# Sixteen weight pieces on ScalarE's queue, a first mixer without order edges, and q and k chains that share tables and roots

## The chip, the cores and the metric

The kernel runs on one core of one Trainium2 chip. The metric is the device time of one execution in microseconds (us), as the median of several runs. Float32 data go through TensorE as float32r, and most operands are split into a high and a low part, so that one product is three matmuls.

## The reference

One decoder layer on x of 1024 tokens by 1024 columns:

```python
x = x + 0.5 * swiglu(rms_norm(x, ffn1_norm), ffn1_w_gate, ffn1_w_up, ffn1_w_down)
h = rms_norm(x, mix_norm)
q, k, v, qi, ki, wi, u = split(h @ w_in)
q = rope(rms_norm(q, q_norm)); k = rope(rms_norm(k, k_norm))
qi = rope(qi); ki = rope(ki)
attn = dsa_attention(q, k, v, qi, ki, wi, top_k=256)
pooled = multiscale_pool(u) @ pool_w * pool_scale
x = x + concat(attn, pooled) @ w_out
x = x + 0.5 * swiglu(rms_norm(x, ffn2_norm), ffn2_w_gate, ffn2_w_up, ffn2_w_down)
```

There are 8 heads of 64. Each query attends to the 256 keys that the indexer (qi, ki, wi) scores highest.

## The kernel before

The tokens are cut into two halves of 512 (h = 0 and 1). FFN 1's gate and up projections run first for both halves (`expand`), and in the same loop the mixer's weights w_in and w_out are split and stored in DRAM as 56 pieces of 128 x 2 x 512 (`p_dr`, by `make_piece`): 8 each for q, k, v and the indexer, 8 for the pooling channels, 16 for the output projection (p_dr 40 to 55). Every later use of a piece is a load by `get_piece` (L229) into a buffer: tag "bw" has 3 buffers, and the first output projection borrows the 4 buffers "sc", which are the softmax tiles of attention as well.

Then the halves are interleaved by Python generators. `fill(main, other)` (L911) advances the main work by a step and then as much of the other work as pays for it. The main work is first `first_mixer` (L951): norm, index projection, scores, `projections` (pooling mixer, k, q, v) with the top-k search, `attention` of half 0, `out_proj` of half 0, then `norm_transposed(0, 2)`. The other work is `down(1)` of FFN 1 and then `second_mixer_opens` (L983), which does the norm, index projection and q, k, v projections of half 1. Later the second mixer is the main work, and FFN 2 fills.

Each engine runs its instructions in one fixed order, which a scheduler writes out when the program is built: it takes instructions by priority as they become ready in its own model of time. `tc.issue_after(mark)` adds an edge that keeps an instruction from being put ahead of `mark` on the mark's engine; on other engines the edge does nothing. In `fill` (L922) the flag `strict[0]` sets such edges: the other work's instructions on TensorE go behind the main work's matmuls of two steps before. `first_mixer` sets the flag at L965, ahead of attention; the second mixer sets it too (L1002). `second_mixer_opens` waits for the flag (L987) before it starts the index projection.

`attention` (L794) takes 4 head pairs in turn, for each 2 blocks of queries and 2 heads: 16 steps for half 0, 8 over 256 keys and 8 over 512. A step is the logits (`lg`, PE), mask and maximum (L823, DVE), exponentials and scaling (L830, L833 on ACT, L834 on DVE), transposes of the probabilities (`tp`, PE), their split (L851 ACT, L852 DVE), the product with the values (`pv`, PE) and its store in `o` (L860 ACT, L861 DVE). The second part of a step runs behind the logits of the next one.

`qk_proj` (L606) multiplies 8 pieces into four banks (`pj`), one for 128 tokens each, and then for each of the four tiles runs a chain: copy from the bank and square (L615, L616, ACT), sums of 64 (L618, DVE), the inverse root of 8 head norms (`rstd_of`: L145, L146, POOL), scaling (L620, DVE), the rotation with a table of gains times cosines and sines made for this tile (L611, POOL; L622 DVE, L623 and L624 POOL, L625 DVE), transposes (`qt`, PE, into the only bank of tag "pv"), split (L630 ACT, L631 DVE) and two stores (L637, SP). The table's tag "st2" has one buffer.

`out_proj` (L518) of half 0 takes 16 pieces, 8 for each half of the columns, into banks `op` of tags ba, ba, bt and pv; 12 matmuls use one piece. The pieces are issued on SP's DMA queue. Behind the sixth piece's matmuls it traces `fetch_x` (L540), which brings half 0's x back in two loads of 1 MB, with an edge behind the last piece's load on SP (`last_sp[0]`). `norm_transposed(0, 2)` squares and scales the four tiles of x and transposes them for FFN 2 (`ba` and `bt`, PE).

Of the kernel before, what the change touches and what calls it, by code (L numbers as in the profile page):

```python
# [10 lines left out]
F32 = mybir.dt.float32  # L11
# [3 lines left out]
AF = mybir.ActivationFunctionType  # L15
ALU = mybir.AluOpType
AX = mybir.AxisListType

S = 1024
D = 1024  # L20
# [4 lines left out]
NH = 8  # L25
HD = 64
# [6 lines left out]
HIGH = 10_000_000  # L33
# [4 lines left out]
def hybrid_layer(ctx: ExitStack, tc: tile.TileContext, x, ffn1_norm, ffn1_w_gate, ffn1_w_up,  # L38
                 ffn1_w_down, mix_norm, w_in, q_norm, k_norm, pool_w, pool_scale, w_out,
                 ffn2_norm, ffn2_w_gate, ffn2_w_up, ffn2_w_down, c_rope, c_diag, c_count, out):  # L40
    nc = tc.nc
# [2 lines left out]
    dr = ctx.enter_context(tc.tile_pool(name="dr", bufs=1, space=bass.MemoryType.DRAM))  # L44

    BUFS = {"XA": 4, "XB": 4, "x8": 4, "w": 5, "qm": 2, "a": 4, "bw": 3, "R": 4, "sc": 4, "mk": 6, "t": 2,
            "st": 4, "sel": 1, "sm": 3, "st2": 1}
    PBUFS = {"fg": 3, "pv": 1, "ba": 2, "bt": 2}
    uid = [0]

    def t(tag, shape, dt=F32, role=None):
        uid[0] += 1
        return sb.tile(shape, dt, name=f"{role or tag}{uid[0]}", tag=tag, bufs=BUFS.get(tag, 1))
# [5 lines left out]
    def f(ap):  # L59
        return ap.bitcast(F32)  # L60
# [23 lines left out]
    ki = sb.tile([128, S], F32R, name="ki")  # L84
    wi = sb.tile([128, 8, 4], F32, name="wi")
    halo = sb.tile([128, 4, 16], F32, name="halo")
    mhalf = sb.tile([128, 8], F32, name="mhalf")
    nc.vector.memset(mhalf, -0.5)
    nc.vector.memset(halo, 0.0)

# [50 lines left out]


    def rstd_of(ss, n, width):
        r = t("st", [128, 8])
        nc.gpsimd.tensor_scalar(r[:, :n], ss, 1.0 / width, EPS, op0=ALU.mult, op1=ALU.add)  # L145
        nc.gpsimd.tensor_tensor(r[:, :n], r[:, :n], mhalf[:, :n], op=ALU.pow)  # L146
        return r
# [78 lines left out]
        for l in range(2):  # L226
            nc.sync.dma_start(p_dr[i][:, l, :a * b], f(part[l][:, :a * b]))

    def get_piece(i, n=512, tag="bw"):  # L229
        w = t(tag, [128, 2, 512], F32R, "bw")  # L230
        last_sp[0] = nc.sync.dma_start(f(w[:, :, :n]), p_dr[i][:, :, :n]).ins
        return w[:, :, :n]


# [283 lines left out]
    def out_proj(h, region, last):  # L518

        mt = {}  # L520
        for k in (4, 5, 6, 7, 0, 1, 2):
            if k % 2 == 0:
                pair = t("X" + region, [128, 2, 2, HALF], F32R)
                n = 1 if k == 2 else 2
                nc.gpsimd.dma_start(pair[:, :n].rearrange("p k l c -> p k (l c)"),
                                    m_dr[h][k:k + n].rearrange("k p l c -> p k (l c)"))
            mt[k] = [pair[:, k % 2, l] for l in range(2)]
        mt[3] = last
        for c in range(2):
            banks = [bank(tag, "op") for tag in ("ba", "ba", "bt", "bt" if h else "pv")]  # L530
            for n, k in enumerate((4, 5, 6, 7, 0, 1, 2, 3)):
                with tc.issue_after(last_raw[0]) if c == 0 and n >= 3 else nullcontext():
                    wt = get_piece(P_O + 2 * k + c, tag="bw" if h else "sc")
                hi, lo = mt[k]
                for i in range(4):
                    tok = slice(i * 128, (i + 1) * 128)
                    mm3(banks[i], hi[:, tok], lo[:, tok], wt[:, 0], wt[:, 1], n == 0, n == NK - 1)
                if c == 0 and n == 5:
                    with tc.issue_after(last_sp[0]):
                        fetch_x(h)  # L540
                yield 0.0 if h else 1.0
            for i in range(4):
                xo = x_at(h, i)[:, c * 512:(c + 1) * 512]
                nc.vector.tensor_add(xo, banks[i], xo)
            yield 1.0
# [59 lines left out]

    def qk_proj(h, hT, cs, which, says, want, home, tags):  # L606
        banks = yield from proj(hT, P_QKV + 8 * which, 512, says, want, tags)
        for i in range(4):
            s = t(home, [128, D], role="qk")
            tab = t("st2", [128, 2, HD])  # L610
            nc.gpsimd.tensor_mul(tab, gqk[:, which], cs[:, i])  # L611
            n = s[:, 512:].rearrange("p (h d) -> p h d", d=HD)
            o = s[:, :512].rearrange("p (h d) -> p h d", d=HD)
            with tc.high_priority(offset=HIGH):
                nc.scalar.copy(s[:, 512:], banks[i])  # L615
            nc.scalar.activation(s[:, :512], s[:, 512:], AF.Square)  # L616
            ss = t("st", [128, 8])
            nc.vector.reduce_sum(ss, o, axis=AX.X)  # L618
            r = rstd_of(ss, 8, HD)
            nc.vector.tensor_mul(n, n, r[:, :, None].to_broadcast([128, NH, HD]))  # L620
            m = t("mk", [128, 512], role="qm").rearrange("p (h d) -> p h d", d=HD)
            nc.vector.tensor_mul(o, n, tab[:, 0:1].to_broadcast([128, NH, HD]))  # L622
            nc.gpsimd.tensor_mul(m[:, :, 0:32], n[:, :, 32:64], tab[:, 1:2, 0:32].to_broadcast([128, NH, 32]))  # L623
# [287 lines left out]
    def fill(main, other):  # L911

        due, marks = 0.0, []
        while True:
            try:
                due += next(main)
            except StopIteration as e:
                return e.value
            marks.append(last_pe[0])
            mark = marks[max(0, len(marks) - 1 - LAG)]  # L920
            while due > 0.0:
                with tc.issue_after(mark) if strict[0] else nullcontext():  # L922
                    got = next(other, None)
                due = 0.0 if got is None else due - got

# [25 lines left out]
    def first_mixer():  # L951
# [9 lines left out]
        for i in range(2):  # L961
            causal_mask(i, masks[i])
        yield from both(projections(0, hT, cs, wanted, 0.0, ("sc", "sc"), MINE), search(0, masks, [2, 3], sc),
                        1.3, 3.0)
        strict[0] = True  # L965
        last = yield from attention(0, masks, "A")
        yield from out_proj(0, "A", last)

# [98 lines left out]
```

## Time and profile before

| | |
|---|---|
| median of 3 runs | 1988.53 us (1986.66 to 1991.15) |
| profiled execution | 1991.77 us, its span 1990.0 us |
| PE busy | 1890.9 us, 95% of the span |
| DVE, ACT, POOL busy | 1182.9, 816.5, 409.1 us |
| mean granted TensorE clock | 0.980 of full speed |

The span is cut into stretches in which the busy time of each engine, the granted clock and the DMA engines' share are read; that shows where TensorE, busy 95% overall, is not. The waits name for each instruction that stood idle what released it. The mean length of an instruction comes from the groups by line and shape. Matmuls overlap, so a matmul's price is the distance from one start to the next rather than its own duration.

### The profile page before, as it was taken

To read this page: it belongs to the slowest core of one execution; us is meant where nothing else is said; L and a number is where in the kernel's file an instruction comes from. 1 tells how busy PE (TensorE), PEld (TensorE's weight loads), DVE (VectorE), ACT (ScalarE), POOL (GpSimd) and SP (SyncE) were. 2 spreads that over 40 slices of the span, in tenths; PEclk is the share of its full clock that TensorE was granted. 3 is DMA by queue.
4 is the path that set the end of the run, shared out by engine and by line. 5 is a ranking of instruction groups with operands and counts; after the bars stand their busy time and mean duration, and the time that the engine had idled before them with its cause. 6 is when DMAs were issued, how large, how long until landed. Compare 5 with 4: busy or idle time off the path is not lost.

```text
span 1990.0 us, 24221 instructions
## 1 busy us (share of the span) xinstructions
PE 1890.9 (95%) x8640; PEld 1558.5 (78%) x8640; DVE 1182.9 (59%) x2204; ACT 816.5 (41%) x1518; POOL 409.1 (21%) x419
## 2 busy tenths in 40 slices
PE   5899999999999999978898999999999999999999
PEld 3688888887878788766676888878888788888887
DVE  6955755654566498646525579997775253444344
ACT  6334333332334254255403458837665133322331
POOL 5654544540001014422412001101100000000000
PEclk9999999999999999988998999999999999999999
DMA  5266656667345736697767544645543542333332
GB/s 158 91 205 211 198 166 200 206 223 288 117 127 167 233 117 203 190 224 182 233 228 213 128 129 130 160 116 118 137 130 101 191 139 85 107 100 89 96 106 74
DMA packets 224393, 314.20 MB, mean 158 GB/s; under 512 B 34192, under 2 KB 143888, under 8 KB 224272
## 3 DMA queue, kind: packets, MB, share of 16 engines
q1 hardware_dynamic: 205904, 281.19, 45.0%
q0 software_dynamic: 18368, 31.46, 7.5%
q8 instruction: 68, 1.11, 0.2%
q14 instruction: 53, 0.43, 0.1%
HBM read 242.84 MB, written 69.76 MB: 157 GB/s over the span
## 4 chain that ended last, share of the span: by engine, by line
PE 86%; DVE 5%; DMA 4%; ACT 2%; POOL 1%; issue 1%; SPq 1%; DVEq 0%; POOLq 0%; ACTq 0%
PE fg L67 30%; PE dn L67 23%; PE pj L67 7%; PE bt L67 6%; PE ba L67 5%; PE pv L67 5%; PE op L67 4%; DMA bw<-p_dr 2%; PE pu L67 2%; PE lg L67 2%; PE tp L70 1%; DVE B L193 1%; DMA rawd<-in_ffn_w_down_dram 1%; DVE w L193 1%; DMA rawa<-a_dr 0%
## 5 line engine op out<-in xcount | busy, mean ns | idle before, releaser
L67 PE MATMUL dn<-wd,a 128*128 128x512 f32 x2112 | 508.0, 395 | 12.5 <-DVE x L455 4.9
L67 PEld LDWEIGHTS dn<-wd,a 128*128 128x128 f32 x2112 | 396.5, 189 | 98.5 <-DVE x L455 6.2
L67 PE MATMUL fg<-XA,w 128*128 128x512 f32 x1056 | 257.4, 393 | 0.0
L67 PE MATMUL fg<-XB,w 128*128 128x512 f32 x1056 | 240.3, 389 | 0.0
L67 PEld LDWEIGHTS fg<-XB,w 128*128 128x128 f32 x1056 | 198.3, 188 | 41.1
L67 PEld LDWEIGHTS fg<-XA,w 128*128 128x128 f32 x1056 | 195.5, 188 | 39.7
L192 ACT CAST w<-rawe 128x512 fp32r<-128x512 f32 x176 | 108.2, 620 | 176.5 <-PE fg L67 120.1
L193 DVE TENSOR_TENSOR w<-x,w 128x512 fp32r<-128x512 f32 x110 | 112.2, 1021 | 113.5 <-ACT w L192 109.0
L193 DVE TENSOR_TENSOR w<-rawe,w 128x512 fp32r<-128x512 f32 x176 | 121.2, 695 | 94.8 <-ACT w L192 94.5
L192 ACT CAST wd<-rawd 128x512 fp32r<-128x512 f32 x176 | 108.0, 620 | 153.0 <-PE dn L67 104.1
L193 DVE TENSOR_TENSOR wd<-rawd,wd 128x512 fp32r<-128x512 f32 x176 | 119.9, 690 | 64.2 <-ACT wd L192 62.3
L67 PE MATMUL fg<-B,w 128*128 128x512 f32 x420 | 105.4, 400 | 13.0 <-DVE B L193 10.0
L455 DVE SCALAR_TENSOR_TENSOR x<-dn,x 128x512 f32<-128x512 f32 x96 | 65.1, 689 | 70.7 <-PE dn L67 70.4
L67 PEld LDWEIGHTS fg<-B,w 128*128 128x128 f32 x420 | 79.7, 192 | 31.7 <-DVE B L193 11.8
L192 ACT CAST p<-praw 128x512 fp32r<-128x512 f32 (+1 forms) x56 | 33.6, 599 | 170.2 <-DMA praw<-in_w_in_dram 70.8
L453 DVE TENSOR_TENSOR x<-dn,x 128x512 f32<-128x512 f32 x96 | 64.0, 686 | 65.4 <-PE dn L67 64.9
L67 PE MATMUL pj<-bw,XB 128*128 128x512 f32 (+1 forms) x384 | 92.6, 392 | 8.3 <-DMA bw<-p_dr 4.5
L193 POOL TENSOR_TENSOR p<-praw,p 128x512 fp32r<-128x512 f32 (+1 forms) x56 | 72.9, 1302 | 134.0 <-ACT p L192 134.0
L67 PE MATMUL ba<-B,w 128*128 128x512 f32 x396 | 94.2, 390 | 0.0
L67 PE MATMUL pj<-bw,XA 128*128 128x512 f32 (+1 forms) x384 | 87.4, 378 | 4.6 <-DMA bw<-p_dr 4.6
L67 PEld LDWEIGHTS pj<-bw,XB 128*128 128x128 f32 x384 | 71.8, 201 | 20.8 <-DMA bw<-p_dr 5.4
L67 PEld LDWEIGHTS ba<-B,w 128*128 128x128 f32 x396 | 74.2, 188 | 15.3
(263 smaller groups left out, 2971.4 us busy)
## 6 DMA issues: line engine op xcount, KB each, us to landing
bw<-p_dr SPq DMA_DIRECT2D x96, 512.0 KB, 4.2
rawd<-in_ffn_w_down_dram SPq DMA_DIRECT2D x88, 512.0 KB, 3.9
p_dr<-p SPq DMA_DIRECT2D x96, 256.0 KB, 2.8
rawe<-in_ffn_w_gate_dram SPq DMA_DIRECT2D x44, 512.0 KB, 4.0
rawe<-in_ffn_w_up_dram SPq DMA_DIRECT2D x44, 512.0 KB, 3.8
x<-in_ffn_w_gate_dram SPq DMA_DIRECT2D x22, 512.0 KB, 5.2
a_dr<-sc SPq DMA_DIRECT2D x44, 256.0 KB, 4.3
x<-in_ffn_w_up_dram SPq DMA_DIRECT2D x22, 512.0 KB, 6.1
```

What stands on the lines that cost most here:

```text
L67: last_pe[0] = nc.tensor.matmul(o, lhs, rhs, start=start, stop=stop, skip_group_check=goes_on).ins
L70: last_pe[0] = nc.tensor.transpose(o, src, ident).ins
L192: nc.scalar.copy(hi, src)
L193: eng.tensor_sub(lo, src, f(hi))
L453: nc.vector.tensor_add(xo, ps, xo)
L455: nc.vector.scalar_tensor_tensor(xo, ps, scale, xo, op0=ALU.mult, op1=ALU.add)
```

## The change

Three edits, and their small needs:

- `get_piece` takes a queue, and the first output projection's 16 pieces are issued by ScalarE's queue (`nc.scalar`) in place of SP's. `last_sp[0]` is then a ScalarE instruction, so the edge that held `fetch_x(0)` behind it on SP no longer acts, nor do the edges to `last_raw[0]` for those pieces.
- In `first_mixer` the flag becomes 1, and `fill` sets edges only for `True`. So the loop that waits for the flag still goes on, and no edges are set in the first mixer.
- `qk_proj` makes one table for all four tiles (128 x 4 x 2 x 64, tag "t") in place of four, and takes the inverse root of two tiles' norms at a time (128 x 16).

```diff
--- before.py
+++ after.py
@@ -44,7 +44,7 @@
     dr = ctx.enter_context(tc.tile_pool(name="dr", bufs=1, space=bass.MemoryType.DRAM))
 
     BUFS = {"XA": 4, "XB": 4, "x8": 4, "w": 5, "qm": 2, "a": 4, "bw": 3, "R": 4, "sc": 4, "mk": 6, "t": 2,
-            "st": 4, "sel": 1, "sm": 3, "st2": 1}
+            "st": 4, "sel": 1, "sm": 3}
     PBUFS = {"fg": 3, "pv": 1, "ba": 2, "bt": 2}
     uid = [0]
 
@@ -84,7 +84,7 @@
     ki = sb.tile([128, S], F32R, name="ki")
     wi = sb.tile([128, 8, 4], F32, name="wi")
     halo = sb.tile([128, 4, 16], F32, name="halo")
-    mhalf = sb.tile([128, 8], F32, name="mhalf")
+    mhalf = sb.tile([128, 16], F32, name="mhalf")
     nc.vector.memset(mhalf, -0.5)
     nc.vector.memset(halo, 0.0)
 
@@ -141,7 +141,7 @@
 
 
     def rstd_of(ss, n, width):
-        r = t("st", [128, 8])
+        r = t("st", [128, 16])
         nc.gpsimd.tensor_scalar(r[:, :n], ss, 1.0 / width, EPS, op0=ALU.mult, op1=ALU.add)
         nc.gpsimd.tensor_tensor(r[:, :n], r[:, :n], mhalf[:, :n], op=ALU.pow)
         return r
@@ -226,9 +226,9 @@
         for l in range(2):
             nc.sync.dma_start(p_dr[i][:, l, :a * b], f(part[l][:, :a * b]))
 
-    def get_piece(i, n=512, tag="bw"):
+    def get_piece(i, n=512, tag="bw", queue=nc.sync):
         w = t(tag, [128, 2, 512], F32R, "bw")
-        last_sp[0] = nc.sync.dma_start(f(w[:, :, :n]), p_dr[i][:, :, :n]).ins
+        last_sp[0] = queue.dma_start(f(w[:, :, :n]), p_dr[i][:, :, :n]).ins
         return w[:, :, :n]
 
 
@@ -530,7 +530,7 @@
             banks = [bank(tag, "op") for tag in ("ba", "ba", "bt", "bt" if h else "pv")]
             for n, k in enumerate((4, 5, 6, 7, 0, 1, 2, 3)):
                 with tc.issue_after(last_raw[0]) if c == 0 and n >= 3 else nullcontext():
-                    wt = get_piece(P_O + 2 * k + c, tag="bw" if h else "sc")
+                    wt = get_piece(P_O + 2 * k + c, tag="bw" if h else "sc", queue=nc.sync if h else nc.scalar)
                 hi, lo = mt[k]
                 for i in range(4):
                     tok = slice(i * 128, (i + 1) * 128)
@@ -605,19 +605,26 @@
 
     def qk_proj(h, hT, cs, which, says, want, home, tags):
         banks = yield from proj(hT, P_QKV + 8 * which, 512, says, want, tags)
+        tabs = t("t", [128, 4, 2, HD], role="tabs")
+        nc.gpsimd.tensor_mul(tabs, cs, gqk[:, which:which + 1].to_broadcast([128, 4, 2, HD]))
+        r = None
+        two = []
         for i in range(4):
-            s = t(home, [128, D], role="qk")
-            tab = t("st2", [128, 2, HD])
-            nc.gpsimd.tensor_mul(tab, gqk[:, which], cs[:, i])
+            if i % 2 == 0:
+                ss = t("st", [128, 16])
+                two = []
+                for e in range(2):
+                    s = t(home, [128, D], role="qk")
+                    two.append(s)
+                    with tc.high_priority(offset=HIGH):
+                        nc.scalar.copy(s[:, 512:], banks[i + e])
+                    nc.scalar.activation(s[:, :512], s[:, 512:], AF.Square)
+                    nc.vector.reduce_sum(ss[:, 8 * e:8 * e + 8], s[:, :512].rearrange("p (h d) -> p h d", d=HD), axis=AX.X)
+                r = rstd_of(ss, 16, HD)
+            s, tab = two[i % 2], tabs[:, i]
             n = s[:, 512:].rearrange("p (h d) -> p h d", d=HD)
             o = s[:, :512].rearrange("p (h d) -> p h d", d=HD)
-            with tc.high_priority(offset=HIGH):
-                nc.scalar.copy(s[:, 512:], banks[i])
-            nc.scalar.activation(s[:, :512], s[:, 512:], AF.Square)
-            ss = t("st", [128, 8])
-            nc.vector.reduce_sum(ss, o, axis=AX.X)
-            r = rstd_of(ss, 8, HD)
-            nc.vector.tensor_mul(n, n, r[:, :, None].to_broadcast([128, NH, HD]))
+            nc.vector.tensor_mul(n, n, r[:, 8 * (i % 2):8 * (i % 2) + 8, None].to_broadcast([128, NH, HD]))
             m = t("mk", [128, 512], role="qm").rearrange("p (h d) -> p h d", d=HD)
             nc.vector.tensor_mul(o, n, tab[:, 0:1].to_broadcast([128, NH, HD]))
             nc.gpsimd.tensor_mul(m[:, :, 0:32], n[:, :, 32:64], tab[:, 1:2, 0:32].to_broadcast([128, NH, 32]))
@@ -919,7 +926,7 @@
             marks.append(last_pe[0])
             mark = marks[max(0, len(marks) - 1 - LAG)]
             while due > 0.0:
-                with tc.issue_after(mark) if strict[0] else nullcontext():
+                with tc.issue_after(mark) if strict[0] is True else nullcontext():
                     got = next(other, None)
                 due = 0.0 if got is None else due - got
 
@@ -962,7 +969,7 @@
             causal_mask(i, masks[i])
         yield from both(projections(0, hT, cs, wanted, 0.0, ("sc", "sc"), MINE), search(0, masks, [2, 3], sc),
                         1.3, 3.0)
-        strict[0] = True
+        strict[0] = 1
         last = yield from attention(0, masks, "A")
         yield from out_proj(0, "A", last)
 
```

The change moves instructions. Three places:

TensorE at the end of the first output projection (`op`: its matmuls; `qt`: transposes of half 1's q; `ba`, `bt`: transposes of half 0's normed x, `sc`; `pj`: here half 1's v projection; `bw`: weight pieces). Before:

```order
L67 MATMUL op1373_8271<-bw1383_8398,mo1346_8063 128x512
L70 MATMUL qt1389_8428<-ident_63,qk1384_8412 128x128 x4
L70 MATMUL qt1396_8454<-ident_63,qk1391_8438 128x128 x4
L70 MATMUL qt1403_8484<-ident_63,qk1398_8468 128x128 x4
L70 MATMUL ba1440_8616<-ident_63,sc1416_8524 128x128
L70 MATMUL ba1443_8644<-ident_63,sc1416_8524 128x128
L70 MATMUL ba1440_8616<-ident_63,sc1425_8550 128x128
L70 MATMUL ba1443_8644<-ident_63,sc1425_8550 128x128
L70 MATMUL qt1410_8510<-ident_63,qk1405_8494 128x128 x4
L67 MATMUL pj1420_8532<-bw1424_8536,XB1081_6759 128x512 x2
```

Now:

```order
L67 MATMUL op1352_8229<-bw1362_8356,mo1325_8021 128x512
L67 MATMUL pj1392_8476<-bw1411_8546,XB1067_6731 128x512 x2
...
L67 MATMUL pj1392_8476<-bw1414_8574,XB1068_6732 128x512 x2
...
L67 MATMUL pj1395_8479<-bw1414_8574,XB1068_6732 128x512 x2
L70 MATMUL qt1369_8390<-ident_63,qk1365_8373 128x128 x4
L70 MATMUL ba1412_8560<-ident_63,sc1388_8468 128x128
L70 MATMUL bt1413_8567<-ident_63,sc1388_8468 128x128
L67 MATMUL pj1395_8479<-bw1414_8574,XB1070_6734 128x512
L70 MATMUL ba1415_8588<-ident_63,sc1388_8468 128x128
```

Before, the transposes of q and of the normed x followed the last output matmul at once, and the whole v projection stood behind them. Now 23 matmuls of the v projection stand between, and the rest of it among the transposes; 36 of its 96 stand ahead of the last 48 output matmuls.

SP's queue around the load of half 0's x (`x` from `x_dr`; `p_dr` 24 to 31 are half 1's index pieces, 8 to 15 k, 0 to 7 q, 40 to 55 the output projection's). Before:

```order
L231 DMA bw1362_8176<-p_dr40_135 128x1024
L231 DMA bw1363_8190<-p_dr42_137 128x1024
L125 DMA x81364_8204<-x_dr0_92 128x2x1024
L125 DMA x81365_8205<-x_dr0_92 128x2x1024
L231 DMA bw1367_8222<-p_dr44_139 128x1024
L231 DMA bw1376_8300<-p_dr6_101 128x1024
L231 DMA bw1368_8236<-p_dr46_141 128x1024
```

Now:

```order
L231 DMA bw1143_7087<-p_dr27_122 128x2x324
L231 DMA bw1144_7101<-p_dr28_123 128x2x324
L231 DMA bw1153_7157<-p_dr29_124 128x2x324
L125 DMA x81343_8162<-x_dr0_92 128x2x1024
L231 DMA bw1168_7228<-p_dr30_125 128x2x324
L231 DMA bw1169_7242<-p_dr31_126 128x2x324
L231 DMA bw1205_7405<-p_dr8_103 128x1024
```

The first half of x is now loaded among the index pieces, early in attention, and the second half behind q's third piece; output pieces no longer stand on this queue. On ScalarE's queue four of them stand among the last softmax steps, and the other twelve behind the copies and squares of half 1's q, with one square among them; the squares of the normed x come behind the last.

TensorE late in attention (`lg`: logits; `tp`: transposed probabilities; `pv`: product with the values; `pj`: here half 1's k projection). Before:

```order
L67 MATMUL pj1218_7432<-bw1284_7780,XB1084_6762 128x512
L67 MATMUL pv1266_7684<-pt1125_6977,XA1230_7504 128x256 x4
L70 MATMUL tp1268_7696<-ident_63,p1253_7622 128x128
...
L67 MATMUL lg1288_7797<-XA1270_7723,qm1273_7729 128x256 x2
L67 MATMUL pv1266_7684<-pt1125_6977,XA1230_7504 128x256
L67 MATMUL lg1289_7801<-XA1270_7723,qm1273_7729 128x256 x2
L67 MATMUL pv1266_7684<-pt1125_6977,XA1230_7504 128x256 x3
L70 MATMUL tp1280_7750<-ident_63,p1261_7667 128x128
...
L67 MATMUL pj1215_7429<-bw1292_7825,XB1082_6760 128x512 x2
```

Now:

```order
L67 MATMUL pv1224_7501<-pt1111_6949,x81155_7172 128x256 x8
L67 MATMUL lg1250_7642<-XA1215_7475,qm1238_7591 128x512 x2
L67 MATMUL lg1251_7646<-XA1215_7475,qm1238_7591 128x512 x2
L67 MATMUL lg1263_7707<-XA1256_7695,qm1259_7701 128x256 x2
L67 MATMUL lg1264_7711<-XA1256_7695,qm1259_7701 128x256 x2
L70 MATMUL tp1253_7657<-ident_63,p1239_7594 128x128
...
L67 MATMUL pv1235_7563<-pt1111_6949,XA1216_7476 128x256 x4
L67 MATMUL lg1274_7769<-XA1256_7695,qm1259_7701 128x256 x2
L67 MATMUL lg1275_7773<-XA1256_7695,qm1259_7701 128x256 x2
L67 MATMUL pv1244_7611<-pt1111_6949,XA1216_7476 128x256 x4
```

Counting such rows: before, 144 projection matmuls of half 1 stood ahead of the logits of the 11th of the 16 steps, and 48 more between there and the 16th. Now 219 stand ahead of the 11th, 63 of them between the 10th and the 11th, and none from the 11th to the 16th.

## Rows read from the trace of the kernel before

**Rows 1.** Stretches: stretch; length, PE, PEld, DVE, ACT, POOL busy (instructions), clock, DMA share, GB/s.

```profile
853.00:900.00 47.00, 33.80 (x201) 29.87 (x200) 23.38 (x66) 23.18 (x59) 9.90 (x16) 0.93 1.06 222
900.00:930.00 30.00, 22.33 (x107) 17.79 (x106) 17.40 (x52) 14.41 (x40) 5.70 (x8) 0.83 0.75 175
930.00:970.00 40.00, 35.79 (x188) 28.46 (x187) 28.89 (x78) 26.98 (x63) 19.83 (x24) 1.00 0.81 217
970.00:1000.00 30.00, 25.17 (x114) 20.30 (x113) 9.04 (x14) 4.87 (x9) 8.64 (x9) 0.89 0.75 248
...
1040.00:1060.00 20.00, 8.00 (x32) 5.25 (x31) 16.05 (x24) 8.62 (x16) 18.09 (x22) 0.64 0.48 135
```

**Rows 2.** Waits, 1040 to 1060: who <- for whom: us in total, times, longest.

```profile
PE qt L70 <- DVE parts L631: 6.8, 3, 4.0
PE qt L70 <- DVE x L544: 3.0, 1, 3.0
```

**Rows 3.** Timeline: start, us, instruction; q's chain of half 1, first and last.

```profile
1032.80 0.59 ACT L615 COPY qk<-pj 128x512 f32<-128x512 f32 x1 [38.79 <-PE pj L67]
...
1053.47 0.69 DVE L625 TENSOR_TENSOR qk<-qk,qm 128x512 f32<-128x512 f32 x1
```

**Rows 4.** Groups by line and shape, POOL, whole span: busy us, mean ns.

```profile
L146 POOL TENSOR_TENSOR st<-st,mhalf 128x8 f32<-128x8 f32 x16 | 28.5, 1780 | 0.8
L811 POOL DMA_DIRECT2D qm<-q_dr x32 | 19.5, 614 | 202.9 <-PE lg L67 141.3 <-PE ba L67 41.4 <-PE tp L70 18.7
...
L611 POOL TENSOR_TENSOR st<-gqk,mk 128x128 f32<-128x128 f32 x16 | 9.9, 619 | 3.6 <-DMA mk<-in_rope_dram 1.4 <-DVE qk L622 1.3
```

**Rows 5.** Waits of PE, 910 to 930.

```profile
PE pv L67 <- DVE ki L597: 3.3, 2, 1.6
PE it L70 <- DVE ki L597: 1.7, 1, 1.7
```

**Rows 6.** Waits, 853 to 900, PE for a weight piece.

```profile
PE pj L67 <- DMA bw<-p_dr: 4.5, 3, 2.0
```

**Rows 7.** DMA issues by kind: count, KB each, median us from issue to landing.

```profile
x<-x_dr SPq DMA_DIRECT2D x4, 1024.0 KB, 8.5
```

**Rows 8.** Groups by line and shape, DVE, 850 to 1060.

```profile
L852 DVE TENSOR_TENSOR pt<-tp,pt 128x512 fp32r<-128x512 f32 x24 | 16.4, 687 | 7.2 <-ACT pt L851 6.8
L823 DVE CUSTOM_DVE_ANT_0 p<-lg,masks 128x512 f32<-128x512 f32 x16 | 10.4, 689 | 10.7 <-PE tp L70 10.5
L861 DVE TENSOR_TENSOR o<-o,pv 64x256 f32<-64x256 f32 x16 | 6.6, 415 | 7.0 <-ACT o L860 6.8
...
L834 DVE TENSOR_SCALAR p<-p,sm 128x512 f32<-128x512 f32 x8 | 4.0, 504 | 0.2
```

**Rows 9.** The same, ACT, 850 to 1060.

```profile
L851 ACT CAST pt<-tp 128x512 fp32r<-128x512 f32 x24 | 14.0, 586 | 17.8 <-PE tp L70 13.9 <-PE pv L67 3.8
L830 ACT ACTIVATE p<-p,sm 128x512 f32<-128x512 f32 x16 | 11.4, 714 | 11.1 <-DVE sm L828 11.1
...
L860 ACT COPY o<-pv 64x256 f32<-64x256 f32 x16 | 5.9, 368 | 9.8 <-PE pv L67 9.5
L833 ACT ACTIVATE p<-p,sm 128x512 f32<-128x512 f32 x8 | 5.8, 723 | 0.4 <-DVE sm L832 0.4
```

**Rows 10.** Timeline of PE in a step over 512 keys.

```profile
898.85 0.60 PE L70 MATMUL tp<-ident,p 128*128 128x128 f32 x4
899.20 1.19 PE L67 MATMUL pv<-pt,XA 128*128 128x256 f32 x8
900.23 2.24 PE L67 MATMUL pj<-bw,XB 128*128 128x512 f32 x9
902.30 1.10 PE L67 MATMUL lg<-XA,qm 128*128 128x512 f32 x4
903.24 0.60 PE L70 MATMUL tp<-ident,p 128*128 128x128 f32 x4
```

**Rows 11.** Timeline of PE behind the stretch 1040 to 1060, from the chain of work.

```profile
1060.41 9.36 PE pj L67 x36
```

## The prediction

> **What bounds the kernel now.** I read the busy times by stretch first, since TensorE (PE) is busy for 95% of the span and only the rest can be won. That rest is dense in one place: from 853 to 1060 us, that is, from half 0's attention to the norm behind its output projection. There PE is idle for 13.2 us in 853-900, 7.7 in 900-930, 4.2 in 930-970, 4.8 in 970-1000, none in 1000-1040 and 12.0 in 1040-1060 [rows 1]. Then I asked the waits what ended these idle times, and the groups by line what an instruction costs. In 1040-1060 PE stood for q's chain: its transposes waited 6.8 us for the split of the tile before (they share one bank) and 3.0 for the output projection's last add [rows 2]. The chain itself ran from 1032.8 to 1054.2 us [rows 3], with POOL busy 18.1 of 20 us [rows 1]. In 900-930 PE waited 3.3 and 1.7 us for the indexer's ki chain on DVE [rows 5]. In 853-900 the DMA share is over 1 [rows 1] and PE waited 4.5 us for weight pieces [rows 6].
>
> The profiled execution took 1991.77 us, 3.2 more than the median of 1988.5. I sum differences read from it and take them off the median. A measurement of this kernel can tell about 0.2%, 4.0 us, from no change: faster means below 1984.5, slower above 1992.5.
>
> **The change part by part.**
>
> *The stretch 1040-1060.* In the new order q's projection ends while 156 of the 192 output matmuls are still to come (36 us at 0.23 us each, the 2.07 us between starts for nine [rows 10]). So q's chain of some 21 us [rows 3] runs beside them, and 23 matmuls of v (5.3 us) cover the last adds and part of the next norm. PE's idle 12.0 us [rows 1] should shrink to about 3: the four norm tiles come one by one, and q's transposes still share one bank. The granted clock, 0.64 in the stretch [rows 1], makes the 36 matmuls behind it take 9.4 us [rows 11] where 36 x 0.23 is 8.3; that 1.1 us goes too. I take -10. Bounds: 0, since no chain gets longer and the order puts only work ahead of it, and -13.
>
> *The ki chain, 900-930.* Three of its four transposes are now followed by 12 or 24 projection matmuls (2.8 or 5.5 us) in place of attention work that waits for DVE. Of the idle 7.7 us [rows 1], 5.0 are that chain's [rows 5]. I take -5; bounds 0, if the pieces for those matmuls land late, and -7.7.
>
> *The output projection's pieces, 970-1000.* On SP each stood behind half 1's pieces and stores. On ScalarE they wait only for their own buffer and an earlier transfer's semaphore. PE is idle 4.8 us in that stretch [rows 1], and not all of it for pieces. I take -2; bounds 0 and -4.8. The Trainium skill ("DMA: Bandwidth & Descriptors", section "Issuing engines are not separate DMA queues") says that transfers issued by several engines share the same 16 DMA engines and interleave, so that only the sequencer's issue time is saved. By that rule this term is 0 and the time 2 us later than I say; the row gives only the idle time and does not decide.
>
> *Half 0's x.* Its edge is gone, and the first megabyte is now issued in the stretch where the DMA share is 1.06 at 222 GB/s [rows 1]. 1.05 MB at that rate are 4.7 us; such a load lands 8.5 us after issue [rows 7]. Two index pieces stand behind it on SP, and PE waits for them in order. I take +3, two thirds of the 4.7, since PE waits for pieces there already [rows 6]; bounds 0 and +8.5. The second megabyte falls where the share is lower (0.75 to 0.81 [rows 1]); nothing.
>
> *Attention without fill.* The last six steps (four over 512 keys, two over 256, which I count as half) lose their projection matmuls, so PE runs at the pace of DVE and ACT. Per 512 keys DVE needs at least 2 x 0.689 + 2 x 0.687 + 0.504 + 0.415 = 3.7 us [rows 8] and ACT 2 x 0.714 + 0.723 + 2 x 0.586 + 0.368 = 3.7 [rows 9]. PE needs 0.94 for the logits, 1.03 for the values and twice 0.35 for the transposes (by starts [rows 10]), 2.7. Five such steps are 18.5 us for ACT and 13.4 for PE. PE idles at least 5 us, I say 8, where it idled 4.2 in 930-970 [rows 1]: +4. Lower bound: -4.2, if the steps overlap with other work after all. Upper bound: PE, DVE and ACT one after the other, 13.4 + 18.4 + 18.5 = 50 us, an idle 37 and +32. I stay near the lower end because the new order keeps two or three steps in flight: logits of the 12th and 13th stand together ahead of the 11th's transposes.
>
> *ScalarE's time.* Sixteen issues at about 0.6 us (POOL's, the nearest row [rows 4]). Four stand among the last softmax steps, 2.4 us; I take +0.5, bounds 0 and +2.4. The other twelve stand where ScalarE has nothing until the norm's squares, and the last is issued when the twelfth piece has been used, four pieces (11 us) ahead of the end.
>
> *Tables and roots.* A root of 128 x 8 takes 1.78 us, a table 0.62 [rows 4]. One root of 16 takes at most two of 8, one table at most four small ones, so POOL has no more to do. A pair's first tile waits for its second: about one copy and square. Half 0's chains lie under FFN 1's down projection and half 1's k under attention, q under the output projection, so nothing; without that cover it is some 2 us a chain.
>
> Sum: -10 - 5 - 2 + 3 + 4 + 0.5 = -9.5, and 1988.5 - 9.5 = **1979 us**. Everything behind the norm is the same work in nearly the same order, and PE is its bound, so the gain is kept. With each term about halfway to its nearer bound, the forecast's own range is 1968 to 1984.
>
> **The rivals.**
>
> *Slower: the bare steps.* One mechanism, late attention: each step's logits, softmax, transposes and values wait for each other more than they overlap. What speaks for it: no projection matmul stands between the logits of the 11th and the 16th step, and 63 stand in one block before it, in which DVE and ACT have little to do. The other terms together are worth -13.5, so it decides when the six steps take more than 13.4 + 4.2 + 13.5 = 31 us. Midway between ACT's 18.5 and the serial 50 is 34 to 36 us: +4 to +5, about 1993, or more. Against: in 930-970, where six steps' parts and half 1's k chain ran at once, DVE was busy 28.9 and ACT 27.0 of 40 us [rows 1], so steps do overlap.
>
> *No change: DMA is the bound of attention.* The share is 1.06, 0.75 and 0.81 in its three stretches [rows 1]. If weight pieces can't come sooner, then pulling projections forward turns ki waits into piece waits (that term 0), the output pieces gain nothing (0), and x costs its full 8.5: -10 + 8.5 + 0.5, with attention's own term at 0 since starved matmuls fill it: 1987 to 1988. The skill's section named above is what one would expect then: another issuing engine, the same 16 engines. For it: 4.5 us of waits for pieces [rows 6]. Against: 0.75 is not full.
>
> *Much faster: attention costs nothing.* Neither x nor the bare steps hurt and the three gains come whole: -13 - 7.7 - 4.8 = -25.5, 1963 us.
>
> *The change does not do what it says:* excluded by the order, which shows the edges gone and the pieces moved.
>
> **How the numbers follow.** Forecast 0.57, bare steps 0.17, DMA bound 0.17, much faster 0.09. Faster by over 0.2%: 0.57 + 0.09 = 0.66; within: 0.17; slower: 0.17. The range reaches from between the much faster case and the forecast, 1965, to the bare steps' decision and a little above, 1994.
>
> **What would show it.** Right: between the output projection's last matmul and FFN 2's first, PE idle falls from 12 us to some 3; the waits of q's transposes for the split and the add are gone; PE's idle in the ki chain is under 3; the output projection runs without waits for pieces. Bare steps: the time from the 11th step's logits to the last values is over 31 us. DMA bound: waits of `pj` for `bw` grow from 4.5 to over 10 us in attention. The forecast is wrong if PE's idle time in attention (13.2 + 7.7 + 4.2 = 25.1 us [rows 1]) grows by more than 6, or if new waits of PE turn up behind the norm.

## The result, and the profile after

The changed kernel took 1965.38 us (median of 3 runs, 1963.88 to 1974.52), before 1988.53: the ratio is 0.990, with a 95% interval of 0.987 to 0.992, so about 20 us less by the ratio (the two medians lie 23.2 us apart). In a second measurement it was 1968.78 us (5 runs, 1966.74 to 1971.92; ratio 0.9903, 0.9889 to 0.9916). The forecast was 1979 us, within 1965 to 1994: the sign is right, the size is about half of what came, and the first median lies at the edge of the range.

The head of the page of the kernel after (span; busy time and share of PE and of the other engines):

```profile
span 1962.1 us, 24169 instructions
PE 1879.0 (96%) x8640; PEld 1554.1 (79%) x8640; DVE 1188.3 (61%) x2204; ACT 816.0 (42%) x1518; POOL 398.0 (20%) x391
```

The stages start elsewhere now, so the two kernels are compared between events: the first logits of half 0's attention, the first output matmul (`op`), the last one, and the first FFN 2 matmul behind the norm. The stretches of before, attention, output projection and norm in turn (columns as in [rows 1]):

```profile
853.00:973.90 120.90, 94.66 (x507) 78.26 (x505) 71.81 (x198) 65.15 (x162) 38.65 (x52) 0.93 0.90 214
973.90:1042.60 68.70, 65.03 (x284) 53.13 (x284) 15.57 (x25) 8.52 (x16) 12.74 (x14) 0.95 0.66 226
1042.60:1087.40 44.80, 32.80 (x149) 26.00 (x149) 23.90 (x35) 16.19 (x29) 15.49 (x20) 0.81 0.66 204
```

The same three of the kernel after:

```profile
844.40:967.00 122.60, 96.41 (x505) 81.96 (x503) 75.19 (x197) 64.71 (x161) 38.60 (x48) 0.87 0.88 228
967.00:1036.90 69.90, 69.86 (x324) 57.69 (x323) 23.83 (x32) 10.16 (x20) 17.69 (x14) 1.00 0.64 220
1036.90:1061.10 24.20, 22.18 (x117) 17.04 (x115) 15.75 (x25) 14.53 (x27) 4.24 (x8) 1.00 0.75 241
```

PE's idle time, length less busy time, goes from 26.2 to 26.2 us in attention, from 3.7 to 0 in the output projection, from 12.0 to 2.0 in the norm: 13.7 us in all. The three stages together last 234.4 and 216.7 us, 17.7 less; the other 4.0 us are busy time. The groups by line and shape show that attention holds the same 228 projection matmuls of half 1 in both kernels, so its lengths can be compared as they stand: 1.7 us longer. The output projection now holds 97 of them in place of 60 and the norm 60 in place of 96, so these two stages are compared together: 113.5 and 94.1 us, 19.4 less.

A wider frame, from the first matmul of FFN 1's down projection to that FFN 2 matmul, before and after:

```profile
478.10:1087.40 609.30, 558.03 (x2588) 459.31 (x2589) 355.34 (x788) 227.57 (x493) 132.93 (x171) 0.96 0.64 189
```

```profile
473.90:1061.10 587.20, 552.24 (x2592) 457.57 (x2592) 359.41 (x787) 227.20 (x493) 120.39 (x143) 0.97 0.64 193
```

It is 22.1 us shorter: 16.3 of idle time and 5.8 of busy time, for the same matmuls at a higher clock. Of the 22.1 us, 4.4 lie ahead of attention's first logits (374.9 and 370.5 us). Everything behind the frame took 902.6 and 901.0 us, with PE idle for 13.1 and 14.8; the waits of PE that are new there are of 1.2 us and less. Ahead of it lie 478.1 and 473.9 us; no edit changes the work of that stage, so 4.2 of the 27.9 us between the two profiled executions are their scatter.

What answers to the waits and groups of before. PE's waits after, 890 to 930 (against [rows 5]):

```profile
PE pj L67 <- DMA bw<-p_dr: 2.5, 1, 2.5
PE pv L67 <- DVE ki L597: 2.5, 1, 2.5
```

In attention (against [rows 6], which covers less), and behind the output projection (against [rows 2]):

```profile
PE pj L67 <- DMA bw<-p_dr: 6.7, 2, 4.2
...
PE bt L70 <- DVE XA L186: 1.4, 2, 1.1
```

Between 967.0 and 1036.9 us the waits of PE are an empty list. POOL's groups after (against [rows 4]):

```profile
L146 POOL TENSOR_TENSOR st<-st,mhalf 128x16 f32<-128x16 f32 x8 | 24.6, 3071 | 0.7
...
L609 POOL TENSOR_TENSOR tabs<-mk,gqk 128x512 f32<-128x512 f32 x4 | 5.0, 1275 | 4.9 <-DMA mk<-in_rope_dram 4.9
```

And q's chain of half 1 (against [rows 3]), its first copy and its last rotation, from ScalarE's and VectorE's timelines:

```profile
991.53 1.13 ACT L620 COPY qk<-pj 128x512 f32<-128x512 f32 x2
...
1011.30 0.69 DVE L632 TENSOR_TENSOR qk<-qk,qm 128x512 f32<-128x512 f32 x1 [0.63 <-POOL qm L631]
```

It takes 20.5 us (21.4 before) but ends 25 us ahead of the end of the output matmuls at 1036.9, where before it ended 12 us behind their end at 1042.6. Run 7 below tests how much of the gain that is.

**The clock.** Stretches of 5 us of before, across the last output matmul at 1042.6 (columns as above):

```profile
1040.00:1045.00 5.00, 2.63 (x12) 1.86 (x10) 3.80 (x7) 0.00 (x0) 4.84 (x6) 1.00 0.00 0
1045.00:1050.00 5.00, 2.17 (x8) 1.40 (x8) 3.77 (x6) 0.59 (x1) 4.80 (x6) 0.57 0.37 87
1050.00:1055.00 5.00, 1.12 (x4) 0.72 (x4) 3.92 (x6) 4.14 (x8) 4.63 (x6) 0.50 1.00 316
1055.00:1060.00 5.00, 2.08 (x8) 1.28 (x9) 4.55 (x8) 3.90 (x8) 3.81 (x6) 0.50 0.54 136
1060.00:1065.00 5.00, 5.00 (x18) 4.03 (x18) 1.77 (x3) 0.59 (x1) 0.00 (x0) 0.73 1.05 340
1065.00:1070.00 5.00, 5.00 (x26) 4.13 (x25) 0.00 (x0) 0.00 (x0) 0.00 (x0) 1.00 1.01 326
```

PE is half idle at full clock (2.4 GHz); the clock is then 0.57 and 0.50 (1.2 GHz) while PE idles on, and full again in the stretch behind the one in which PE was busy throughout. In the kernel after it is 1.00 in both stretches from 967.0 to 1061.1.

### The profile page after: what moved, and what is told of

Read it like the earlier page. It is cut to its first block, busy times and chain, and to the rows that moved or that the text cites. A ratio compares the mean times of both kernels' runs of the same rounds, so it can differ in the third digit from the quotient of the medians.

```text
span 1962.1 us, 24169 instructions
## 1 busy us (share of the span) xinstructions
PE 1879.0 (96%) x8640; PEld 1554.1 (79%) x8640; DVE 1188.3 (61%) x2204; ACT 816.0 (42%) x1518; POOL 398.0 (20%) x391
## 4 chain that ended last, share of the span: by engine, by line
PE 88%; DVE 4%; DMA 4%; ACT 1%; POOL 1%; issue 1%; SPq 1%; POOLq 0%; ACTq 0%
PE fg L67 31%; PE dn L67 24%; PE pj L67 7%; PE bt L67 6%; PE ba L67 5%; PE pv L67 5%; PE op L67 4%; PE pu L67 2%; PE lg L67 2%; PE tp L70 2%; DMA bw<-p_dr 1%; DVE B L193 1%; DMA XA<-k_dr 1%; DMA rawd<-in_ffn_w_down_dram 1%; DVE w L193 0%
## 5 line engine op out<-in xcount | busy, mean ns | idle before, releaser
L67 PE MATMUL ba<-B,w 128*128 128x512 f32 x396 | 94.1, 390 | 0.0
L67 PEld LDWEIGHTS pj<-bw,XB 128*128 128x128 f32 x384 | 71.3, 201 | 23.2 <-DMA bw<-p_dr 7.7
```

Of the source, the lines that this page charges most:

```text
L67: last_pe[0] = nc.tensor.matmul(o, lhs, rhs, start=start, stop=stop, skip_group_check=goes_on).ins
```

## The experiments

Twelve runs. Edits are against the kernel after unless said; "us" is the median, the ratio is to runs of the kernel before made beside it, with its 95% interval; runs are compared with each other by this ratio. The first three undo parts, to see whether the parts add up.

**1. Edges edit alone.** (The kernel before with this.)

```diff
-                with tc.issue_after(mark) if strict[0] else nullcontext():
+                with tc.issue_after(mark) if strict[0] is True else nullcontext():
...
-        strict[0] = True
+        strict[0] = 1
```

> The kernel before with the order edges of the first mixer taken away, and nothing else. Theory (the gain is the v projection's matmuls that now cover the end of half 0's output projection and the norm behind it): PE's idle between the first output matmul and FFN 2's first falls from about 16 us to under 5, and the median lies at 1968 to 1974, most of the change. Rival 1 (ScalarE's queue carries it): 1980 to 1988, with PE waiting for pieces in the output projection. Rival 2 (the shorter q chain carries it): 1980 to 1988, with PE still waiting for q's transposes.

1974.41 us, 0.9929 (0.9911 to 0.9947): 14 us less, at the edge of what was expected. PE's idle time in the norm is 2.0 us (24.90 less 22.91), with pieces on SP and small roots. So this edit alone covers the end of the norm; the output projection keeps 4.2 us of idle time (75.80 less 71.59), so the two together have 6.2, where under 5 was expected.

**2. Queue and joint edits, edges as before.**

```diff
-                with tc.issue_after(mark) if strict[0] is True else nullcontext():
+                with tc.issue_after(mark) if strict[0] else nullcontext():
...
-        strict[0] = 1
+        strict[0] = True
```

> The changed kernel with the order edges put back, so that ScalarE's queue and the joint tables and roots are left. Theory (cover by v): 1980 to 1987, because q's transposes and the norm again follow the last output matmul with nothing between; the shorter chain saves 2 to 4 us there and the queue up to 4. Rival 1 (queue): 1966 to 1972. Rival 2 (chains): 1970 to 1976.

1981.78 us, 0.9964 (0.9952 to 0.9976), as expected.

**3. Joint tables and roots alone.** (Run 2 with the queue edit taken back.)

```diff
-                    wt = get_piece(P_O + 2 * k + c, tag="bw" if h else "sc", queue=nc.sync if h else nc.scalar)
+                    wt = get_piece(P_O + 2 * k + c, tag="bw" if h else "sc")
```

> The kernel before with the joint tables and roots alone. Theory: 1984 to 1988; q's chain stays exposed behind the output projection and gets 1 to 4 us shorter, since POOL made a table for each tile there. Rival 2 (the chains carry the gain): under 1978.

1984.84 us, 0.9981 (0.9972 to 0.9990): 3.8 us, where the prediction had nothing. The queue edit (run 2 against run 3) is worth 3.4 us, plus or minus 3.0, with half 0's early x in it, since that comes with the edit. PE waited only 0.6 us for output pieces in either run, so this gain is not shown to be theirs.

**4. Edges in attention, none from the output projection on.**

```diff
-        strict[0] = 1
+        strict[0] = True
         last = yield from attention(0, masks, "A")
+        strict[0] = 1
         yield from out_proj(0, "A", last)
```

> The changed kernel with the edges set during attention and taken away again from its output projection on: the projections are spread over the steps as before, and v still covers the end. Theory (my terms: bare steps +4, ki chain -5, so attention is even): 1963 to 1969, attention's length within 3 us of the changed kernel's. Rival 3 (the six bare steps cost a lot): 1953 to 1960. Rival 4 (the ki chain's gain is real and bare steps cost nothing): 1970 to 1975.

1964.93 us, 0.9881 (0.9862 to 0.9900): as fast as the change. Attention is 6.5 us shorter than in the change (116.1 and 122.6 us), more than the 3 us expected, and the stages behind it are longer by as much (100.5 and 94.1). What the order inside attention becomes is no source of the gain.

**5. Half 0's x held back.** `last_sp[0]` keeps the last piece issued on SP, so x is loaded between q's fourth and fifth piece, around 964 us.

```diff
-        last_sp[0] = queue.dma_start(f(w[:, :, :n]), p_dr[i][:, :, :n]).ins
+        got = queue.dma_start(f(w[:, :, :n]), p_dr[i][:, :, :n]).ins
+        if queue is nc.sync:
+            last_sp[0] = got
```

> The changed kernel, but the load of half 0's x is held behind the last piece on SP again (it lands between q's third and fourth piece, some 70 us later than in the changed kernel). My theory (the early megabyte takes DMA time from pieces that PE waits for, +3): this kernel is 3 us faster than the changed one, 1962 us (1960 to 1964), and PE's waits for pieces of the projections in the attention stretch, 6.7 us in the changed kernel, fall by about 3. Rival (the load is hidden): the same as the changed kernel, 1964 to 1967. Second rival: x comes too late for the output projection's additions, 1967 or more, with a wait for x8 on DVE near 1030 us.

1972.42 us, 0.9918 (0.9899 to 0.9937). Not faster; against the second measurement of the change (run 9) the difference in ratio is 0.0015, plus or minus 0.0023, and not resolved. PE's waits for pieces in attention were 8.5 us, not less than 6.7.

**6. The output pieces back on SP** (x is then late too, and later than in run 5).

```diff
-                    wt = get_piece(P_O + 2 * k + c, tag="bw" if h else "sc", queue=nc.sync if h else nc.scalar)
+                    wt = get_piece(P_O + 2 * k + c, tag="bw" if h else "sc")
```

> The changed kernel, but the sixteen output pieces are issued by SP again (with that x is held back too, so it is to be compared with the run that only holds x back). My theory (pieces stand behind other work on SP, worth 2): 2 us slower than that run, and PE waits some 2 us for pieces in the first output projection, where the changed kernel had none. Rival (the same 16 DMA engines serve either queue, so the issuing engine decides nothing): the same time as that run within 1 us, no new waits for pieces.

1975.65 us, 0.9928 (0.9915 to 0.9941): 3.2 us slower than run 5, though the ratios of the two overlap (the difference is 2.0 us, plus or minus 4.6); against run 9 the difference in ratio is 0.0025, plus or minus 0.0019. PE's waits in the output projection of run 6, 973.7 to 1050.3:

```profile
PE op L67 <- DMA bw<-p_dr: 6.8, 3, 3.4
```

and of run 5, 968.1 to 1038.8:

```profile
PE op L67 <- DMA bw<-p_dr: 2.9, 2, 2.4
```

SP's timeline of run 6 shows what stands in the queue beside the pieces: stores of k (`k_dr<-parts`) that wait for their data, and half 0's x:

```profile
969.52 1.72 SPq L231 DMA_DIRECT2D bw<-p_dr  x3
972.40 6.45 SPq L644 DMA_DIRECT2D k_dr<-parts  x4
979.90 10.48 SPq L231 DMA_DIRECT2D bw<-p_dr  x5
...
1007.43 0.94 SPq L125 DMA_DIRECT2D x<-x_dr  x2
1008.46 31.09 SPq L231 DMA_DIRECT2D bw<-p_dr  x13
```

and PE's timeline its longest wait:

```profile
1018.98 2.52 PE L67 MATMUL op<-bw,XA 128*128 128x512 f32 x8 [3.40 <-DMA bw<-p_dr]
```

That wait is not behind the stores: the last of them was issued at 996 us. It comes behind x's two loads, which stand among the output pieces here and ahead of them in run 5 (963.90). So this pair of runs moves x as well as the pieces and does not isolate the queue. The queue alone does not decide the waits either: in the kernel before, with the pieces on SP and x among them, PE's wait for pieces between 973.9 and 1042.6 is 1.2 us, and in run 1 it is 1.8 us (967.6 to 1043.4); in run 4, with the pieces on ScalarE, it is 3.2 us:

```profile
PE op L67 <- DMA bw<-p_dr: 1.2, 1, 1.2
```

```profile
PE op L67 <- DMA bw<-p_dr: 1.8, 2, 1.6
```

```profile
PE op L67 <- DMA bw<-p_dr: 3.2, 1, 3.2
```

The landing differs as well. DMA issues of run 6 (960 to 1045), then of the kernel after (955 to 1035), median us to landing last:

```profile
bw<-p_dr SPq DMA_DIRECT2D x27, 512.0 KB, 5.5
```

```profile
bw<-p_dr ACTq DMA_DIRECT2D x16, 512.0 KB, 3.8
```

**7. Edges from the output projection on, none in attention**: the complement of run 4.

```diff
         last = yield from attention(0, masks, "A")
+        strict[0] = True
         yield from out_proj(0, "A", last)
```

> The changed kernel, but the edges are set again from the first output projection on, and only there; attention has none. With this order the last output matmul has no v projection before it, as in the kernel before, while the six last attention steps are bare, as in the changed kernel. My theory (the gain of the edges lies in what covers the end of the output projection and the norm behind it): 10 to 13 us slower than the changed kernel, 1975 to 1979 us, PE idle between the last output matmul and the first FFN 2 matmul is 10 to 14 us again. Rival (the gain lies in attention, where projections come sooner): 1964 to 1968 us.

1987.82 us, 0.9989 (0.9978 to 1.0): by ratio 17 us slower than run 9, plus or minus 3.5, more than either theory said. Its output projection and norm:

```profile
970.40:1037.40 67.00, 63.89 (x287) 51.89 (x285) 14.26 (x24) 9.18 (x18) 8.28 (x6) 0.97 0.64 214
1037.40:1085.00 47.60, 34.62 (x151) 27.39 (x152) 25.31 (x35) 17.08 (x31) 13.26 (x17) 0.78 0.61 191
```

Idle 3.1 and 13.0 us, with the clock down to 0.78. The two stages last 114.6 us, 94.7 in run 9. PE waits for q's chain again:

```profile
PE qt L70 <- DVE qk L632: 5.0, 1, 5.0
PE qt L70 <- DVE parts L638: 4.5, 1, 4.5
```

Runs 2, 4, 7 and 9 are a square, all with the queue and joint edits:

| ratio to before | edges behind attention | none behind attention |
|---|---|---|
| edges in attention | 0.9964 (run 2) | 0.9881 (run 4) |
| none in attention | 0.9989 (run 7) | 0.9903 (run 9) |

A step to the right is worth 0.0083 and 0.0086, 17 us. A step down costs 0.0025 (plus or minus 0.0016) and 0.0022 (plus or minus 0.0023), 4 to 5 us; the second alone is not resolved.

**8. Edges in both attentions, none from each output projection on.** To run 4 this adds, in the second mixer:

```diff
         last = yield from attention(1, masks, "B")
+        strict[0] = 1
         yield from out_proj(1, "B", last)
```

> Edges set in both attentions, and off from each output projection on (of the run with edges in the first attention alone, 1964.9 us, it differs in the second output projection, where FFN 2's down matmuls now stand among the output matmuls). My theory (work free of dependences among the output matmuls covers waits for pieces and for the last softmax; PE waited 4.1 us for pieces in the second output projection of the changed kernel): 2 to 4 us faster, 1961 to 1963 us. Rival (the down matmuls spent there are missing behind the second output projection, and the same idle time turns up at the end): 1964 to 1967 us.

1959.19 us, 0.9844 (0.9821 to 0.9866): faster than both kernels, and by 7.4 us, plus or minus 5.9, than run 4. Behind the first norm it took 893.0 us, run 4 898.5. The stretch around the second output projection's start in run 4, with a wait of 3.2 us for a piece in it, and in run 8, where the down matmuls fill it:

```profile
1500.00:1520.00 20.00, 16.82 (x81) 13.91 (x80) 3.10 (x5) 2.06 (x4) 1.84 (x2) 0.92 0.35 125
```

```profile
1500.00:1520.00 20.00, 20.00 (x109) 17.22 (x108) 5.58 (x10) 3.51 (x7) 1.86 (x2) 1.00 0.21 71
```

**9. The change again**, as the partner of runs 10 and 11 (no edit).

> The changed kernel again, beside the next two on one chip. If holding back half 0's x really costs time (the run that did so took 1972.4 us), this is 1964 to 1967 us; if that difference was the scatter of a median of three, this is 1968 to 1973.

1968.78 us, 0.9903 (0.9889 to 0.9916). Its median lies in the second case, scatter; what x costs stays open between a gain of 3 us and a loss of 3.

**10. A table and a root for each tile, queue and edges as changed** (`qk_proj` and `rstd_of` as before).

```diff
-            if i % 2 == 0:
-                ss = t("st", [128, 16])
...
-                r = rstd_of(ss, 16, HD)
...
+            ss = t("st", [128, 8])
+            nc.vector.reduce_sum(ss, o, axis=AX.X)
+            r = rstd_of(ss, 8, HD)
```

> The changed kernel with a table for each tile and a root for each tile, as before; queue and edges as changed. Theory A (the joint roots and tables save POOL time that ends up in PE's, as the run of that edit alone seems to show with 3.8 us): 3 to 4 us slower than the changed kernel run beside it. Theory B (my prediction: in the new order v covers q's chain and attention covers k's, so the length of a chain decides nothing): within 1 us of it.

1977.88 us, 0.9949 (0.9935 to 0.9962): 9 us slower than run 9, plus or minus 3.8, beyond both theories. From FFN 1's down projection to FFN 2's first matmul it took 600.4 us, run 9 590.7, with PE idle for 42.4 and 36.3. Of these 6.1 us of idle time, 2.4 lie ahead of the first logits and 3.9 in the output projection, where run 9 has no wait and run 10 has these (979.5 to 1053.3):

```profile
PE qt L70 <- DVE parts L631: 2.5, 1, 2.5
PE op L67 <- DMA bw<-p_dr: 1.9, 2, 1.5
```

A wait for the same split stands in run 1, the other kernel with small roots and v at the end (967.6 to 1043.4):

```profile
PE pv L67 <- DVE parts L631: 2.6, 1, 2.6
```

The chain waited for is half 1's k, not q. Run 10's timelines, PE's wait and SP's stores of k and of q:

```profile
984.98 0.66 PE L70 MATMUL qt<-ident,qk 128*128 128x128 f32 x4 [2.47 <-DVE parts L631]
```

```profile
979.76 7.61 SPq L637 DMA_DIRECT2D k_dr<-parts  x4
...
1059.97 0.93 SPq L637 DMA_DIRECT2D q_dr<-parts  x2
```

In run 10 a transpose of k waits for the split of the tile before, in run 1 a product with the values (`pv`), since both use the only bank of tag "pv". The last rotation of k ends 2.2 us behind the first output matmul in the change, 4.7 in run 10 and 5.4 in run 1. So k's chain outlasts attention, and with small roots something waits for it; q's chain makes nothing wait in the output projection of either.

Run 6 against run 1 is the same edit with the pieces on SP: both have the edges edit, and run 6 has the joint tables and roots besides. There it is worth 0.2 us, plus or minus 4.4. So what the joint edit gives depends on the other edits.

**11. Run 4 with x held back** (the edit of run 5).

> Edges in the first attention, none from the output projection on (1964.9 us), and half 0's x held back behind the last piece on SP. Theory A (my prediction's: an early x delays pieces that PE waits for): 1 to 3 us faster, 1962 to 1964 us. Theory B (the run that held x back in the changed kernel was slower, since two loads of 1 MB late in attention stand ahead of v's pieces and beside the output pieces): 3 to 7 us slower, 1968 to 1972 us, with waits of op for pieces above the 3.2 us that the run without it had.

1962.58 us, 0.9873 (0.9858 to 0.9888), 2.3 us below run 4 and inside its interval. PE waited for no piece in the first output projection.

**12. Runs 8 and 11 together.**

> Edges in both attentions and off from each output projection on (1959.2 us), and half 0's x held back (2.3 us faster where that was tried with edges in the first attention). If the two gains lie in different places and add up: 1956 to 1958 us. If the run with the late x was faster by chance: 1959 to 1961 us. PE should wait for no pieces in the second output projection, and for none in the first.

1958.75 us, 0.9846 (0.9829 to 0.9862); one of its six runs took 7282.67 us, which nothing here explains. Against run 8 the difference is 0.4 us, plus or minus 5.5, too wide to tell whether the two gains add. PE waited for no piece in either output projection, as expected. Run 8 stays the best that can be told apart.

## Why the prediction was right in sign and half in size

One path through the runs leads to the change (its steps add up by construction, since each run is the next one's partner): joint tables and roots (run 3) -3.8 us, output pieces on ScalarE with the early x (run 2) -3.4, no edges in attention (run 7) +5.0, none behind it (run 9) -17.1; together -19.3. Other paths give other shares: without the joint edit, edges and queue are worth 10 us (run 10) and edges alone 14 (run 1).

By stage, the profile shows which terms came out. In attention the ki chain, x and the bare steps sum to +2, and it became 1.7 us longer for the same matmuls. For the output projection and the norm the sum has -12, and they became 19.4 us shorter. Another 4.4 us lie ahead of attention, where the sum has nothing.

- **The stretch 1040-1060, -10:** the mechanism was right, the size was not. Idle time went from 12.0 to 2.0 us as foreseen, and q's waits are gone. But lifting the edges there is worth 17 us (runs 2 and 4, 7 and 9). This is the mis-sized term, and two things were left out of it. One is the clock, which I charged with the 1.1 us of the 36 matmuls behind the stretch, while the transposes and norm inside it ran at 1.2 GHz too and the output projection was at 0.95: in the two stages PE's busy time fell by 5.8 us. The other is the output projection's own idle time of 3.7 us: I counted it under the pieces, but only 1.2 us of it were waits for pieces, and the rest waits on attention's end and k's chain, which the same projection matmuls cover. How the 17 us divide between the two is not settled.
- **The ki chain, -5:** it shrank to 2.5 us from 5.0, half of what I took, since one of its waits stays.
- **Output pieces on ScalarE, -2:** not shown. The queue edit, which moves x as well, gave 3.4 us (plus or minus 3.0, run 2 against run 3) and 5.0 (plus or minus 3.7, run 9 against run 6), but with small roots and no edges it came out as a loss of 4.0 (plus or minus 4.5, run 10 against run 1). PE's waits for output pieces were 0.6 to 6.8 us with the pieces on SP and 0 to 3.2 with them on ScalarE. The Trainium skill ("DMA: Bandwidth & Descriptors", section "Issuing engines are not separate DMA queues") makes the issuing engine worth only its issue time; no pair of runs here moves the pieces without x, so none decides that.
- **Half 0's early x, +3:** not shown. Holding it back cost 3.0 us by ratio in one order (run 5 against run 9) and saved 1.6 in another (run 11 against run 4), neither beyond its interval (4.6 and 4.8).
- **Bare attention steps, +4:** right in direction and too small. From the 11th step's logits to the first output matmul of the kernel after:

```profile
926.10:967.00 40.90, 27.02 (x129) 21.38 (x128) 33.69 (x75) 23.78 (x59) 15.19 (x20) 0.79 0.72 209
```

  PE idles 13.9 of 40.9 us, where I said 8, while DVE is busy for 33.7. That is past the 31 us at which the slower rival was to decide. It did not: ahead of these steps attention idles 12.3 us in the kernel after, while in the kernel before 20.9 of its 26.2 us fell ahead of 930. So the idle time moved to the late steps and did not grow, and the end was worth 17 us rather than 10. The square's 4 to 5 us are the price of taking the edges out of attention as a whole, and what the ki chain gains is already taken off in them. In run 7, where the steps are bare and the end is not covered, no gain is left: 1987.8 us.
- **Tables and roots, 0:** wrong. Alone they gave 3.8 us (run 3), with both other edits 9.1 (run 10 against run 9), with the edges edit alone nothing that can be told (run 6 against run 1). The assumption that failed is "half 1's k under attention, so nothing": k's chain runs on into the output projection, and in both kernels with small roots and without edges a transpose of k or a product with the values waits 2.5 us for it (runs 10 and 1), in the change none. That and the pieces explain 3.9 of the 9 us. Most of the rest lies ahead of attention, which begins 378.1 us into run 10's frame and 371.0 into run 9's; but in run 1, with the same small roots, it begins at 373.1, so this is not settled. Nor is where the 3.8 us of run 3 lie: in its one profiled execution 1.7 us are ahead of FFN 2's first matmul and the rest behind it, where the kernels with the same second mixer took 898 to 904 us.
- **ScalarE's time, +0.5:** not seen. An issue took 0.33 us, not 0.6, the twelve later ones stand behind the squares as read, and PE waited for none of them.

The rival that DMA bounds attention falls: PE's waits for pieces there did grow, to 6.7 and 7.7 us (before 4.5), but not above 10, and its idle time in attention did not grow. The much faster case gave the right number for the wrong reason, since attention did cost something. One figure does not follow from its rule: half the way to the nearer bound is 9.7 us over all terms, which makes the forecast's own range 1969 to 1989 and not 1968 to 1984.

## What to carry to other kernels

An idle stretch of PE costs more than its idle time, since the granted clock fell to half with it here: price a cover from both. Here the edges that pace filling work paid in attention and cost where the main work ends: kept in attention and dropped from the output projection on, in both mixers, it gave the best kernel here that can be told apart, 1959.19 us. And a chain is hidden only as far as the in-order instructions that wait for it stand late enough: price it at the place where its consumer now stands.

## What was not expected of the hardware

A root of 128 x 16 on POOL takes 3.07 us where one of 128 x 8 took 1.78: 1.7 times the time for twice the width, so joining saves 0.5 us for a pair; one table of 128 x 512 takes 1.28 us where four of 128 x 128 took 2.5. The same 512 KB load landed in 3.8 us (median) from ScalarE's queue and in 5.5 from SP's, in the same stage of two kernels that differ in the queue and in when x is loaded. SP's landing in the kernel before was 4.7 us in that stage (965 to 1045), so what sets it stays open.
